# Two-layer hybrid encoder on one core: TensorE in emission order inside both attention stages

## The chip, the cores and the metric

The kernel runs on 1 core of one Trainium2 chip. The metric is the device time of one execution in microseconds (us); a kernel's time is the median over its runs.

## The reference

The program computes two transformer-like layers on a sequence of 1024 frames and 1024 channels. Each layer normalizes, mixes along the sequence, projects out with a gated residual, and runs a SwiGLU network. Only the mixers differ (cut):

```python
# layer 0
q, k, v, u = split(h @ w_in)
a_out = chunked_relpos_attention(q, k, v)   # 8 heads of 64, own + 8 earlier 64-frame chunks, softmax
b_out = s5_mixer(u)                         # complex diagonal scan, gelu, gate y * sigmoid(y @ w_glu)
x = x + g1 * (concat([a_out, b_out]) @ w_out)
x = x + g2 * swiglu(h2)
# layer 1
c_out = retention_mixer(cq, ck, cv, cg)     # 4 heads of 128, chunk recurrence, group norm, swish gate
d_out = stick_breaking_mixer(dq, dk, dv)    # 8 heads, 128-query blocks:
    # z = q @ k.T * scale; w = exp(log_sigmoid(z) + reverse cumsum of -softplus(z)); out = w @ v
x = x + g1 * (concat([c_out, d_out]) @ w_out)
x = x + g2 * swiglu(h2)
```

## The kernel before

All weights are multiplied at full precision by three passes: a weight tile is loaded as `raw` by SP, ACT casts it to its high part (line 141) and POOL or DVE subtracts to get the low part (line 142), into tiles named `whl` or `wo`; `mm3` then issues three matmuls per product (lines 248 to 250). PSUM has three tags: `mm` with 3 banks, `at` with 4, `av` with 1.

The program is written as generators on a clock of ticks (class Pipe, line 51). A generator yields a number n and is resumed n ticks later; a tick first resumes those that are due, in the order in which they were queued, then starts new ones. That sets the **emission order**: the order in which the program's text calls the instructions of each engine. Line 1541 opens the program with `schedule_with_timeline_sim=True`: a scheduler with its own simulated timeline then picks the order in which each engine gets its instructions. In the kernel before it does so for all engines, everywhere.

The first attention stage (`ab_phase`, layer 0) runs one a_unit a tick, for 64 pairs of head and 128-query block; the first three ticks lie in the stage before it. An a_unit is:

```python
sc, n = self.scores(self.mm_bank, ...)      # L498 on PE; L597, L600 on DVE: bias, row minimum
yield 1
nc.scalar.activation(pw, pw, AF.Exp, ...)   # L605 on ACT
yield 2
pts = self.flip(pool, pw, W // P)           # L510 transposes on PE, L512 copies on ACT
...                                         # even head: done
yield 1
self.weigh(av, ...)                         # L521 on PE, both heads of a pair
```

`weigh` is issued with the odd head alone, for both heads, and every fourth block ends with four transposes (L626) of a factor that POOL spreads (L619). Beside it an s5_block is started every fifth tick, 8 in all (L955 transposes of `u`, which a DMA brings, L964, L985, L987, L1002 on PE, most of the rest on DVE), and from step 46 on the gate's projection `glu`.

The second (`cd_phase`, layer 1) runs 32 periods of four ticks. Each period starts one d_unit (stick-breaking attention: query loads L483; four ticks later scores L498 into three `at` banks, mask add L1185 on DVE, two sigmoids L1188 and L1189 on ACT; one tick later two scans L1197 and a product L1199 on DVE; three ticks later nine transposes of `flip`; one tick later, odd heads, 18 matmuls of `weigh`) and one c_tile (retention: four ticks after its start a projection of 24 matmuls in four parts of one tick each; `ra`, `rb` on DVE, L1078 and L1079; `cr` on POOL, L1084; transposes L1089; `qkt`, `ckd` L1091 to L1094; L1097, L1099 on PE; `cat`, `cst`, L1101 and L1108, on DVE; L1112, L1114 on PE; statistics L1117, L1118 on DVE and L1119, L1120 on POOL; L1122 on DVE, which frees the `at` bank). Before it, `d_dense` (L1151) makes queries and keys, written to memory and loaded again from there.

Of the kernel before, what the change touches and what calls it, by code (L numbers as in the profile page):

```python
# [1368 lines left out]
def build(ctx, tc, I, out):  # L1369
    k = Trunk(ctx, tc, I, out)  # L1370
    nc, pipe = tc.nc, k.pipe
    k.cond()


    with tc.tile_pool(name="pp", bufs=1, reuse_waits="tile") as pp:
        with tc.tile_pool(name="first", bufs=1, reuse_waits="tile") as xp:
            k.first(pp, xp)
        with tc.tile_pool(name="heads", bufs=1, reuse_waits="tile") as hp:
            with tc.tile_pool(name="qk", bufs=1, reuse_waits="tile") as qp:
                right = ExitStack()  # L1380
                sp = right.enter_context(tc.tile_pool(name="set0", bufs=1, side="right", reuse_waits="tile"))
                k.stream.low = nc.vector
                for n, _ in enumerate(k.a_dense(qp)):
                    if n == 2:
                        setup = k.s5_setup(sp)
                        pipe.start(setup)
                    if n in (19, 32):
                        pipe.start(k.ada(qp, 0, 2 if n == 19 else 4))
                    if n == 38:
                        k.a_open(hp)  # L1390
                    if n == 46:
                        assert setup.gi_frame is None
                        right.close()
                        ap = right.enter_context(tc.tile_pool(name="mixa", bufs=1, side="right", reuse_waits="tile"))
                        k.pp = pp
                    pipe.tick(*([k.a_step(hp, ap, n - 46)] if n >= 46 else []))
                k.stream.low = nc.gpsimd
                pipe.tick(k.a_step(hp, ap, 2))
            k.ab_phase(hp, ap, 3)
            right.close()  # L1400
            k.pp = None
    with tc.tile_pool(name="xp0", bufs=1, reuse_waits="tile") as xp:
        x = [xp.tile([P, T], F32, name=f"x{n}") for n in range(NK)]
        for n in range(NK):
            nc.sync.dma_start(out=x[n], in_=I["x"][n])
        pipe.start(k.ada(xp, 0, 3))
        k.out_proj(xp, 0, x, [0, 1, 2, 4, 5, 6, 7, 3], 5, [(0, 4), (0, 3)], [k.ada(xp, 0, 5)])

        def done(n, h):
            if h:  # L1410
                nc.sync.dma_start(out=k.xd[n], in_=x[n])
            k.stat(xp, x[n], n, h)
            if n == NK - 1:
                pipe.start(k.norm(xp, x, h, [(1, 1), (1, 0)]))

        k.ffn(xp, 0, x, done, [lambda l=l, p=p: k.ada(xp, l, p) for l, p in ((1, 1), (1, 0), (1, 2), (1, 4), (1, 3))])
        for t in range(4):
            pipe.tick(k.v_tile(xp, "hf", k.wdv, t))
            pipe.tick()
        pipe.drain()  # L1420


    with tc.tile_pool(name="dense1", bufs=1, reuse_waits="tile") as dp:
        for n, _ in enumerate(k.d_dense(dp)):
            pipe.tick()
            if n == 1:
                for t in range(4, NT):
                    pipe.tick(k.v_tile(dp, "ve", k.wdv, t))
                    pipe.tick()
                k.wdv.free()  # L1430
    right = ExitStack()
    cp = right.enter_context(tc.tile_pool(name="mixc", bufs=1, side="right", reuse_waits="tile"))
    with tc.tile_pool(name="mixd", bufs=1, reuse_waits="tile") as dp:
        k.c_setup(cp)
        k.cd_phase(dp, cp)
    with tc.tile_pool(name="xp1", bufs=1, reuse_waits="tile") as xp:
        x = [xp.tile([P, T], F32, name=f"x{n}") for n in range(NK)]
        for kk in (0, 1, 2, 4, 5, 6):
            pipe.tick(k.mix_split(kk))
        pipe.tick(k.mix_split(3, 512))  # L1440
        for n in range(NK):
            nc.sync.dma_start(out=x[n], in_=k.xd[n])
        pipe.tick()
        while k.tail.gi_frame is not None:
            pipe.tick()
        right.close()
        k.out_proj(xp, 1, x, [0, 1, 2, 4, 5, 6, 7, 3], 1, [(1, 4), (1, 3)], [k.ada(xp, 1, 5)])

        def done(n, h):
            nc.sync.dma_start(out=out[n, :, h * 512:h * 512 + 512], in_=x[n][:, h * 512:h * 512 + 512])  # L1450

        k.ffn(xp, 1, x, done)
# [93 lines left out]
```

## Time and profile before

| | us |
|---|---|
| median of 3 runs | 2639.24 (2636.28 to 2641.58) |
| the profiled execution | 2628.13 |
| its span | 2626.3 |
| PE busy in the span | 2535.4 (97%) |
| PE weight loads busy | 2104.9 (80%) |
| DVE, ACT, POOL busy | 1134.9 (43%), 708.9 (27%), 809.5 (31%) |

The span is the time between the first and last instruction of the one profiled execution; 1.8 us of that execution lie around it. In the rows below, PE is TensorE's matmuls, PEld its weight loads (beside the matmuls), DVE VectorE, ACT ScalarE, POOL GpSimd, SP SyncE, which issues DMAs. A matmul with float32 operands has more records than instructions: each matmul of `weigh` shows as two.

### The profile page before, as it was taken

How to read it: one execution, taken by the hardware profiler on the slowest of the kernel's cores; microseconds unless marked ns; L12 is line 12 of the kernel's file. 1: busy time of each engine (PE TensorE's matmuls, PEld its weight loads, DVE VectorE, ACT ScalarE, POOL GpSimd, SP SyncE). 2: the span in 40 equal slices, each digit the busy share in tenths (PEclk: the TensorE clock that was granted, in tenths of full speed). 3: DMA queues.
4: the chain of work that ended last, by engine and by line, in shares of the span. 5: the costliest groups of instructions: out<-in, count | busy, mean ns of one | idle time of the engine just before them, and what ended most of it. 6: DMA issues, size and time to landing. Idle time of an engine off the chain costs nothing. (4 is left out here: it accounts for less than half of the span.)

```text
span 2626.3 us, 32531 instructions
## 1 busy us (share of the span) xinstructions
PE 2535.4 (97%) x12912; PEld 2104.9 (80%) x12912; DVE 1134.9 (43%) x2058; ACT 708.9 (27%) x1293; POOL 809.5 (31%) x538
## 2 busy tenths in 40 slices
PE   6999898999999999999999999999999999999999
PEld 4898776777888888888788778887788888888887
DVE  6576563474333322222531566765632222222223
ACT  4332568322111111111232444544231111111100
POOL 3465003423222222232212143423243333333311
PEclk9999999999999999999999999999999999999999
DMA  7287764543233311111234333224311111111101
GB/s 282 92 248 211 211 179 154 184 145 108 93 113 112 113 49 48 48 49 49 87 109 145 87 104 102 68 76 156 112 65 49 49 50 49 50 50 49 49 9 64
DMA packets 145479, 267.12 MB, mean 102 GB/s; under 512 B 34416, under 2 KB 82224, under 8 KB 144560
## 3 DMA queue, kind: packets, MB, share of 16 engines
q1 hardware_dynamic: 145328, 265.05, 31.7%
q8 instruction: 102, 1.67, 0.3%
q14 instruction: 49, 0.40, 0.1%
HBM read 221.22 MB, written 45.88 MB: 102 GB/s over the span
## 5 line engine op out<-in xcount | busy, mean ns | idle before, releaser
L249 PE MATMUL mm<-HT,whl 128*128 128x512 f32 x1744 | 680.3, 390 | 4.5 <-DVE HT L351 4.4
L248 PE MATMUL mm<-HT,whl 128*128 128x512 f32 x1744 | 680.7, 391 | 1.8 <-ACT HT L350 1.5
L250 PE MATMUL mm<-HT,whl 128*128 128x512 f32 x1744 | 679.8, 390 | 0.0
L142 POOL TENSOR_TENSOR whl<-raw,whl 128x1024 fp32r<-128x1024 f32 x136 | 332.5, 2453 | 494.5 <-ACT whl L141 487.8
L249 PEld LDWEIGHTS mm<-HT,whl 128*128 128x128 f32 x1744 | 327.7, 188 | 76.4 <-DVE HT L351 6.7
L248 PEld LDWEIGHTS mm<-HT,whl 128*128 128x128 f32 x1744 | 327.7, 188 | 72.8 <-ACT HT L350 2.8
L250 PEld LDWEIGHTS mm<-HT,whl 128*128 128x128 f32 x1744 | 327.9, 188 | 68.5
L1342 DVE SCALAR_TENSOR_TENSOR x<-at,col,x 128x512 f32<-128x512 f32 x352 | 262.4, 750 | 268.6 <-PE at L250 268.4
L1327 DVE TENSOR_TENSOR sg<-sg,mm 128x512 f32<-128x512 f32 x88 | 60.4, 687 | 642.3 <-PE mm L250 642.3
L249 PE MATMUL at<-aT,wo 128*128 128x512 f32 x704 | 274.9, 390 | 1.9 <-POOL aT L1329 1.9
L250 PE MATMUL at<-aT,wo 128*128 128x512 f32 x704 | 274.8, 390 | 0.0
L248 PE MATMUL at<-aT,wo 128*128 128x512 f32 x704 | 273.1, 391 | 0.0
L248 PE MATMUL mm<-whl,HT 128*128 128x512 f32 (+1 forms) x688 | 249.5, 363 | 8.6 <-ACT HT L402 8.1
L249 PE MATMUL mm<-whl,HT 128*128 128x512 f32 (+1 forms) x688 | 244.8, 356 | 0.0
L142 POOL TENSOR_TENSOR wo<-raw,wo 128x1024 fp32r<-128x1024 f32 x44 | 107.4, 2464 | 442.4 <-ACT wo L141 442.4
L250 PE MATMUL mm<-whl,HT 128*128 128x512 f32 (+1 forms) x688 | 242.1, 357 | 0.0
L141 ACT CAST whl<-raw 128x1024 fp32r<-128x1024 f32 x154 | 161.3, 1054 | 172.3 <-PE mm L250 164.7
L1329 POOL TENSOR_TENSOR aT<-sg,aT 128x512 fp32r<-128x512 f32 x88 | 115.2, 1309 | 289.6 <-DVE aT L1328 281.9
L1326 ACT ACTIVATE sg<-mm 128x512 f32<-128x512 f32 x88 | 52.6, 598 | 518.7 <-PE mm L250 518.7
L141 ACT CAST wo<-raw 128x1024 fp32r<-128x1024 f32 x44 | 44.0, 1046 | 494.2 <-PE at L250 488.0
L248 PEld LDWEIGHTS mm<-whl,HT 128*128 128x128 f32 x688 | 138.0, 201 | 25.7 <-ACT HT L402 10.7
L249 PEld LDWEIGHTS at<-aT,wo 128*128 128x128 f32 x704 | 132.2, 188 | 30.8 <-POOL aT L1329 2.4
(295 smaller groups left out, 3193.0 us busy)
## 6 DMA issues: line engine op xcount, KB each, us to landing
raw<-in_ffn_w_in SPq DMA_DIRECT2D x88, 512.0 KB, 3.5
raw<-in_ada_w SPq DMA_DIRECT2D x80, 512.0 KB, 4.0
raw<-in_ffn_w_out SPq DMA_DIRECT2D x44, 512.0 KB, 3.4
ada<-in_ada SPq DMA_DIRECT2D x16, 512.0 KB, 10.2
qkd<-stk SPq DMA_DIRECT2D x32, 256.0 KB, 4.8
q<-qkd SPq DMA_DIRECT2D x64, 128.0 KB, 3.9
ks<-qkd SPq DMA_DIRECT2D x32, 256.0 KB, 4.3
qkd<-stk SPq DMA_DIRECT2D x16, 512.0 KB, 3.2
```

The source lines that it names most:

```text
L141: nc.scalar.copy(hi, u.raw[:, :u.n])
L142: self.low.tensor_sub(lo, u.raw[:, :u.n], hi.bitcast(F32))
L248: mm(out, lhs.hi, rhs.hi, start=start, stop=False)
L249: mm(out, lhs.hi, rhs.lo, start=False, stop=False)
L250: mm(out, lhs.lo, rhs.hi, start=False, stop=stop)
L1326: nc.scalar.activation(sg, gu[0], AF.Silu)
L1327: nc.vector.tensor_mul(sg, sg, gu[1])
L1329: nc.gpsimd.tensor_sub(a[m].lo[:, sl], sg, a[m].hi[:, sl].bitcast(F32))
L1342: nc.vector.scalar_tensor_tensor(xh, ps, self.col[layer, 5][:, n:n + 1], xh, M, A)
```

## The change

Two calls are put into a context in which the order of one engine, PE, is not picked by the scheduler: it gets its instructions in emission order. All other engines are ordered by the scheduler as before, and so is PE outside of the two calls.

```diff
-            k.ab_phase(hp, ap, 3)
+            with tc.manual_schedule(engines={nc.tensor.engine}):
+                k.ab_phase(hp, ap, 3)
...
-        k.cd_phase(dp, cp)
+        with tc.manual_schedule(engines={nc.tensor.engine}):
+            k.cd_phase(dp, cp)
```

PE has the same matmuls in both kernels, and their order differs only in the two stages and in the first matmuls of the output projection behind each. Names with a number at the end are buffers; a row is an instruction, or several alike.

**Head of layer 1, PE.** `mm_10971` in the change is the last projection of d_dense; `mm_11216` before is the third of three projections of c_tiles (`mm_11064`, `mm_11127`, `mm_11216`, 72 matmuls in all, from which the last three stand here) that follow d_dense directly. Before:

```order
L248 MATMUL mm_11216<-whl_10904,HT_540 128x512
L249 MATMUL mm_11216<-whl_10904,HT_540 128x512
L250 MATMUL mm_11216<-whl_10904,HT_540 128x512
L498 MATMUL at_11047<-ks_11016,q_11038 128x128 x2
L498 MATMUL at_11053<-ks_11016,q_11038 128x512 x2
```

With the change:

```order
L248 MATMUL mm_10971<-HT_540,whl_10716 128x512
L249 MATMUL mm_10971<-HT_540,whl_10716 128x512
L250 MATMUL mm_10971<-HT_540,whl_10716 128x512
L498 MATMUL at_11052<-ks_11021,q_11043 128x128 x2
L498 MATMUL at_11058<-ks_11021,q_11043 128x512 x2
L498 MATMUL at_11061<-ks_11021,q_11043 128x512 x2
L248 MATMUL mm_11069<-whl_10780,HT_246 128x512
```

The first unit's scores moved from behind the 72 projection matmuls to ahead of them. SP's order up to the loads of that unit's queries is the same in both.

**Middle of layer 0, PE.** Before:

```order
L498 MATMUL mm<-ks,q 128x320 x2
L955 MATMUL at<-ident,u 128x128 x4
L521 MATMUL av<-pts,v 64x128
L498 MATMUL mm<-ks,q 128x320 x2
L521 MATMUL av<-pts,v 64x128 x5
L498 MATMUL mm<-ks,q 128x320 x2
L521 MATMUL av<-pts,v 64x128
L498 MATMUL mm<-ks,q 128x320 x6
```

With the change:

```order
L498 MATMUL mm<-ks,q 128x320 x4
L510 MATMUL at<-ident,pw 128x128 x5
L1002 MATMUL at<-ident,yg 128x128 x4
L498 MATMUL mm<-ks,q 128x320 x4
L510 MATMUL at<-ident,pw 128x128 x5
L521 MATMUL av<-pts,v 64x128 x10
```

Each weigh now stands in one piece; between the transposes of its own odd head and it stand one unit's scores and one unit's transposes. Over the whole program the matmuls of weigh stand in 101 separate runs before and in 49 with the change.

**A period of layer 1, PE.** `at_12306` is the third bank of scores of a d_unit, `mm_12419` a c_tile's projection. Before, the first two banks of these scores (`at_12297`, `at_12303`) stand ahead of that projection, and the third near its end:

```order
L249 MATMUL mm_12419<-whl_11907,HT_509 128x512
L498 MATMUL at_12306<-ks_11815,q_12211 128x448 x2
L250 MATMUL mm_12419<-whl_11907,HT_509 128x512
L510 MATMUL at_12327<-ident_69,b_12161 128x128 x4
L510 MATMUL at_12334<-ident_69,b_12161 128x128 x4
```

With the change, the same unit's three banks in a row:

```order
L498 MATMUL at_12302<-ks_11820,q_12216 128x256 x2
L498 MATMUL at_12308<-ks_11820,q_12216 128x448 x2
L498 MATMUL at_12311<-ks_11820,q_12216 128x448 x2
L248 MATMUL mm_12319<-whl_11033,HT_246 128x512
L249 MATMUL mm_12319<-whl_11033,HT_246 128x512
```

All three banks of scores are now issued together, ahead of the projection. Table loads on ACT, which its order shows too, are 16 before and 14 with the change.

**Head of layer 0, PE**, in words: before, 12 matmuls of scores, the transposes of `u` (L955), L964 and ten transposes of flips come before the first weigh. With the change the first weigh stands right behind L955, two matmuls of scores and three transposes; L964 and the rest follow it.

## Rows read from the trace of the kernel before

**Rows 1.** Windows by stretch: us, busy us of each engine, PEclk, DMA share, GB/s.

```profile
300.00:407.00 107.00, 97.72 (x815) 79.68 (x814) 73.07 (x266) 65.65 (x161) 5.01 (x5) 0.98 0.68 181
407.00:465.00 58.00, 50.76 (x334) 38.84 (x333) 17.63 (x59) 54.15 (x94) 23.94 (x17) 1.00 0.47 152
...
600.00:1000.00 400.00, 396.89 (x1778) 326.99 (x1778) 151.15 (x199) 57.08 (x68) 119.15 (x61) 1.00 0.29 92
1442.00:1458.00 16.00, 16.00 (x73) 13.24 (x72) 2.77 (x7) 3.68 (x7) 5.23 (x4) 1.00 0.83 222
1458.00:1482.00 24.00, 18.97 (x113) 15.27 (x112) 16.14 (x27) 12.14 (x31) 2.35 (x3) 0.86 0.19 54
1482.00:1792.00 310.00, 299.95 (x1891) 250.71 (x1890) 214.27 (x395) 150.05 (x372) 117.29 (x106) 0.98 0.28 83
```

**Rows 2.** Timeline of PE, head of layer 1: start us, us, instruction, idle before.

```profile
1442.30 0.39 PE L248 MATMUL mm<-whl,HT 128*128 128x512 f32 x1
...
1458.62 1.48 PE L498 MATMUL at<-ks,q 128*128 128x128 f32 x8
```

**Rows 3.** Line 483 on SP, 1450.5 to 1454.3: four query loads.

```profile
L483 SPq DMA_DIRECT2D q<-qkd x4: 574/586/614, 1450.8 to 1453.6; - x4
...
DMA to landing us min/median/max: 4.9/6.1/7.0
```

**Rows 4.** Timeline of PE at the head of layer 0.

```profile
279.43 1.11 PE L955 MATMUL at<-ident,u 128*128 128x128 f32 x4 [1.89 <-DMA u<-ud]
...
285.56 0.94 PE L521 MATMUL av<-pts,v 128*64 128x128 f32 x12
```

**Rows 5.** Line 487 on SP, 270 to 290: three value loads.

```profile
L487 SPq DMA_DIRECT2D v<-vd x3: 430/602/602, 279.0 to 284.2; - x3
...
DMA to landing us min/median/max: 4.8/4.8/5.4
```

**Rows 6.** Timeline of PE in layer 1: two runs of weigh.

```profile
1577.67 0.43 PE L521 MATMUL av<-pts,v 128*64 128x128 f32 x2
...
1578.25 0.98 PE L498 MATMUL at<-ks,q 128*128 128x384 f32 x4
...
1587.23 0.54 PE L521 MATMUL av<-pts,v 128*64 128x128 f32 x5
...
1589.34 0.97 PE L498 MATMUL at<-ks,q 128*128 128x384 f32 x4
```

**Rows 7.** Lines by shape, 300 to 407: busy us, mean ns.

```profile
L597 DVE CUSTOM_DVE_ANT_0 pw<-mm,abias 128x320 f32<-128x320 f32 x38 | 17.9, 483 | 4.0 <-PE mm L498 1.9 <-PE at L510 1.9
...
L605 ACT ACTIVATE pw<-pw,ast 128x640 f32<-128x640 f32 x18 | 14.9, 831 | 8.3 <-DVE ast L600 8.1
L512 ACT COPY pts<-at 128x512 f32<-128x512 f32 x24 | 13.9, 580 | 8.4 <-PE at L510 7.1 <-PE av L521 1.2
...
L512 ACT COPY pts<-at 128x128 f32<-128x128 f32 x24 | 6.3, 272 | 0.5 <-PE at L510 0.5
```

**Rows 8.** Lines of ACT, 407 to 465.

```profile
L605 ACT ACT_TABLE_LOAD x4 | 5.1, 1283 | 0.1
```

**Rows 9.** Lines of DVE and POOL, 1482 to 1792.

```profile
L1197 DVE TENSOR_TENSOR_SCAN w<-one,w 128x384 f32<-128x384 f32 (+7 forms) x56 | 82.6, 1475 | 19.7 <-ACT w L1188 19.6
...
L1084 POOL TENSOR_TENSOR cr<-ra,rb 128x256 f32<-128x256 f32 x28 | 43.1, 1540 | 180.7 <-DVE rb L1079 134.6 <-PE at L498 43.9 <-PE mm L521 2.1
...
L142 POOL TENSOR_TENSOR whl<-raw,whl 128x1024 fp32r<-128x1024 f32 x16 | 39.7, 2499 | 4.4 <-ACT whl L141 4.4
L1199 DVE TENSOR_TENSOR b<-b,w 128x1151 f32<-128x1151 f32 x28 | 37.7, 1348 | 0.5
...
L1094 DVE TENSOR_SCALAR ckd<-cr,c_kd 128x128 f32<-128x128 f32 x28 | 16.1, 574 | 0.8 <-POOL cr L1084 0.7
...
L1079 DVE TENSOR_TENSOR rb<-mm,ccs 128x256 f32<-128x256 f32 x28 | 11.5, 412 | 0.0
...
L1122 DVE TENSOR_SCALAR co<-at,cmv 128x128 f32<-128x128 f32 x28 | 11.3, 405 | 14.2 <-POOL cmv L1120 13.8
```

## Prediction, made before the change was run

> **What bounds the kernel now.** I read the windows of the two stages first, for what PE does there, then PE's timeline at the two heads of the stages and at two runs of `weigh`, then the rows of DVE, ACT and POOL from which a PE in a fixed order would have to wait.
>
> The windows show PE at work nearly all the time: 97.72 of 107 us in the middle of layer 0's attention, 50.76 of 58 in its second part, 299.95 of 310 in layer 1's [rows 1]. No other engine is full, except ACT in the second part of layer 0's (54.15 of 58) [rows 1]. So time is gained where PE's own time shrinks or its few idle microseconds go, and lost where PE stands before an instruction whose inputs are late while others behind it could run. The second is what a scheduler avoids and what a fixed order allows. Idle time of PE in these windows: 9.3 + 7.2 us in layer 0 and 10.0 in layer 1, 26.5 in all. A busy PE isn't a PE at its peak, so gains beyond the idle time are possible too.
>
> **The sum, part by part.** It stands against the profiled execution's 2628.13 us; the median of the runs shown is 2639.24, 11.1 us above it, and I add that at the end.
>
> 1. *Head of layer 1.* Before, d_dense is followed at 1442.30 by 72 projection matmuls of three c_tiles, and the first scores start at 1458.62 [rows 2]. Those scores read queries whose four loads SP issues from 1450.8 to 1453.6 and which land 4.9 to 7.0 us later, so about 1457 to 1458.5 [rows 3]. The projections thus fill just the time in which the queries are on their way: PE is busy for all of the 16 us [rows 1]. In the change the scores come directly behind d_dense. SP's order up to these loads is unchanged, and what SP waits for there (d_dense's results and free `raw` buffers) doesn't come sooner. PE then idles from 1442.5 to 1458.5: +16.0. The 72 matmuls come later and can cover what was open then: in 1458 to 1482 PE was busy for 18.97 of 24 us [rows 1], so 5.0 come back. **+11**. Bounds: +19, if nothing comes back and the loads land 3 later for DMAs that collide; +6, if the loads land 5 sooner, since the 72 matmuls no longer run beside d_dense's last evacuations and the weight casts.
>
> 2. *Head of layer 0.* Before, the transposes of `u` start when it lands, at 279.43, and the first weigh at 285.56 [rows 4]; its values are loaded from 279.0 on and land 4.8 us later, at 283.8 to 284.4 [rows 5]. Between the two PE issued scores, L964 and flips. In the change the first weigh stands right behind L955, so that some 30 matmuls which ran before the values landed come after: 12 of 320 to 512 columns, 8 of L964, 6 transposes, about 4 us. The loads of `u` and the values are issued one DMA (0.6 us) earlier. **+3**, bounds 0 to +6.
>
> 3. *Fewer runs of weigh.* Two weigh matmuls alone (two records each) take from 1577.67 to 1578.25, 0.58 us; sixteen in a run take 2.11 us, from 1587.23 to 1589.34 [rows 6]. The difference, 1.53, over the 14 more is 0.11 each, so that a run costs 0.36 us beyond its matmuls. The profile shows weigh on 128*64 tiles and its neighbours on 128*128. The change has 49 runs for 101, so 52 fewer. At 0.30 each, since some runs stand beside L964, which has 128*64 as well: **-16**; at 0.25 to 0.36, -13 to -19.
> The Trainium skill, TensorEngine Tiling (Array Packing), Key Properties, says that a change of the tiling mode drains TensorE. By it every run saved would be worth something, which speaks for this term; it gives no figure, and the term goes by the rows.
>
> 4. *Table loads.* Two of ACT's are gone, 1.28 us each [rows 8], in a stretch where ACT is at 93%: **-2.6**, 0 if ACT isn't waited for.
>
> 5. *Waits that the new order leaves.* The 26.5 us of idle PE in the windows [rows 1] are waits of the old order, and the old order is gone: **-26.5**; bound 0, if what is late (exp, reduction, sigmoids) is late in any order. I take them as gone because the new waits are counted from zero in the next part.
>
> 6. *Waits that the new order brings*, each behind one instruction on PE, with all of PE behind it:
>  - Weigh of layer 0. Between an odd head's transposes and its weigh stand one unit's four score matmuls (0.6 us) and five transposes (0.55). In that 1.15 us ACT must copy the transposes out, 0.58 + 0.27 = 0.85; if an exp of 0.83 is ahead, 1.68 [rows 7]. So 0 to 0.55 and latencies: 0.35 on each of 30, 10.5. Bounds 0 and 30 x 0.6 = 18.
>  - Scores of layer 0. They need a free `mm` bank; a reduction of 0.48 [rows 7] empties one and a unit takes two. DVE was busy 73 of 107 us [rows 1], with the s5 work ahead of the reduction at times. 0.13 on each of 57, 7.5; bounds 0 and 57 x 0.25 (half a reduction) = 14.
>  - Third bank of scores in layer 1. It is the bank that L1122 frees. From the end of a projection to there stand: `ra`, `rb` 0.82, `cr` 1.54, `ckd` 0.57, two scans 2.95, the product 1.35, L1122 0.41 [rows 9], and seven small instructions of DVE and POOL, at most 0.41 each, for which I take 0.34: 10.0 us. PE comes to it, after an even period, when it has issued the rest of that period: 24 projection matmuls at 0.225 (72 in 1442.30 to 1458.62 [rows 2]), 5.4; nine transposes, 1.0; three banks of scores, 1.0; six small ones, 1.2; and two banks of the next, 0.7: 9.3. So 0.7 on each of 16: 11. After an odd period PE has 18 weigh matmuls, 2 us, more to do, and doesn't wait. Bounds 0 and 16 x 1.1 (one more small DVE instruction ahead), 18. The scheduler has just this bank's matmuls half a period later.
>  - POOL's `cr` in layer 1. The subtraction of a weight tile, 2.50 us, stands 16 times among the 28 `cr` [rows 9]. Where it is ahead of one, `cr` and PE's L1089 are late by up to 2.5 less the slack of two ticks; 0.5 on each of 16, 8. Bounds 0 and 16.
>  Together **+37**, bounds 0 and +66.
>
> Sum: 11 + 3 - 16 - 2.6 - 26.5 + 37 = +5.9. On the median: 2639.2 + 5.9 = **2645 us**. All ends low: 6 + 0 - 19 - 2.6 - 26.5 + 0 = -42; all high: 19 + 6 - 13 + 0 + 0 + 66 = +78. Neither is likely, as the terms are independent.
>
> **The rivals.**
> - *The waits of part 6 stay small* (faster). Ticks give each dependence a fixed distance, and for all but the third bank the distance is about what the rows ask for. If half an exp or a subtraction is seldom in the way, 37 becomes 15: 5.9 - 22 = -16, **2623**. It decides from new waits of 31 us in all, 0.35 for each of 61 steps and 28 periods; below that the change gains. For it: ACT has 61% load in 300 to 407 and 48% in layer 1, DVE 68% and 69% [rows 1]. Against: their chains are long, and the idle rows show PE waiting already.
> - *PE's weight loads are the room* (faster). The windows show PEld at 118.5 of 165 us in layer 0, 72%, at 250.7 of 310, 81%, in layer 1, and at 327.0 of 400, 82%, in the dense work [rows 1]. If an order in large pieces lets both stages run as the dense work does, they take 118.5/0.82 = 144.5 and 250.7/0.82 = 305.7 us: -20 and -4; with both heads' +14, **2629**. The Trainium skill, Perfetto Trace Analysis, Identifying the Most-Contended Engine, says that weight-load busy time and not matmul busy time tells how much room TensorE has; by that rule layer 0 has more room than its 16.5 us of idle PE.
> - *Waits at their upper ends* (slower). The gate's stretch, where ACT has 93%, starves every weigh and the chain of the third bank meets POOL's subtractions: 66 for 37, +35, **2674**. It decides from 0.6 us per step.
> - *Even.* The heads cost 14 and the runs give 16; new waits equal the old ones, within 5 us: **2639**. 0.2%, 5.3 us, is about what a measurement of this kernel can tell from no change.
> - *The order isn't what bounds it*, so that all is hidden. PE's order is shown to change and PE is full, so 2 in 100.
>
> **How the numbers follow.** Forecast (+6 to +25) 0.30, waits small 0.25, room in the weight loads 0.11, even 0.21, upper ends 0.11, no effect 0.02. Faster: 0.25 + 0.11 = 0.36. Same: 0.21 + 0.02 = 0.23. Slower: 0.30 + 0.11 = 0.41. The signs are near even, so the range takes in both: down to **2617**, a little under the waits-small case, and up to **2669**, a little under the upper ends. The forecast alone would reach from 2643 to 2664.
>
> **What would show it.** Right, step by step: PE idle about 16 us before the first L498 of layer 1, released by a query DMA; a wait of the first L521 of layer 0 on a value DMA; PE waits at L521 on ACT L512, at L498 on DVE L597, at L498 of layer 1 on DVE L1122, some 16 of them of 0.7; runs of L521 in one piece that cost 0.3 beyond their matmuls; windows of the two stages in which PE's time is less by some 8 us each and its idle time about 10 us more. Wrong: the windows of both stages shorter with idle time below 26 us (then the first rival), or PEld over 80% in layer 0 (then the second), or a head without the 16 us.

## The result, and the profile after

| | before | with the change |
|---|---|---|
| median, us (runs) | 2640.41 (4) | 2658.38 (4) |
| lowest to highest, us | 2636.28 to 2643.53 | 2656.98 to 2661.75 |
| ratio | | 1.0071, 95% interval 1.0053 to 1.0088 |
| span of the profiled execution, us | 2626.3 | 2656.9 |
| mean granted clock of it | 0.992 | 0.981 |

The change makes the kernel slower by 18 us, 0.7%, and the whole interval (0.5 to 0.9%) lies above no change. The time is within the forecast's range, at three times the loss that was forecast (18 us for 5.9).

PE in the whole span, from the page (busy us, share, instructions). Before it was 2535.4 us:

```profile
PE 2527.8 (95%) x12912; PEld 2111.2 (79%) x12912; DVE 1142.6 (43%) x2058; ACT 702.8 (26%) x1291; POOL 788.4 (30%) x538
```

So PE was busy for 7.6 us less, in a span that is 30.6 us longer. Three of the windows of [rows 1] after the change, and 1442 to 1482 in one piece (us, busy time of PE, weight loads, DVE, ACT, POOL, then the granted clock, DMA share, GB/s):

```profile
300.00:407.00 107.00, 89.76 (x779) 75.03 (x777) 66.82 (x249) 63.06 (x153) 4.82 (x5) 0.97 0.69 178
407.00:465.00 58.00, 43.14 (x300) 35.29 (x301) 19.78 (x73) 43.41 (x81) 18.25 (x12) 0.88 0.52 159
1442.00:1482.00 40.00, 24.13 (x107) 19.65 (x105) 3.46 (x5) 7.98 (x10) 9.50 (x4) 0.86 0.60 172
1482.00:1792.00 310.00, 295.85 (x1903) 252.06 (x1904) 219.41 (x395) 143.73 (x373) 91.64 (x101) 0.97 0.28 81
```

In 300 to 407 PE has 17.2 us without work, where [rows 1] had 9.3; in 407 to 465 14.9 for 7.2, with the clock at 0.88; at the head of layer 1 15.9 of 40. Layer 1's body is near the old one, 14.2 for 10.0. (The windows are the same times, not quite the same work: layer 1 starts some 24 us later in the change.)

The two heads. Before, PE's order had other work there [rows 2, 4]; now its timeline (start, duration, instruction, idle time before it and what ended it) shows the stalls. Layer 0, then layer 1:

```profile
278.82 1.12 PE L955 MATMUL at<-ident,u 128*128 128x128 f32 x4 [5.79 <-DMA u<-ud]
...
284.81 0.69 PE L521 MATMUL av<-pts,v 128*64 128x128 f32 x2 [3.80 <-DMA v<-vd]
```

```profile
1482.54 2.56 PE L498 MATMUL at<-ks,q 128*128 128x128 f32 x6 [16.41 <-DMA q<-qkd]
```

What PE waited for (total us, times, longest), in layer 0's attention, 268 to 480:

```profile
PE mm L248 <- ACT whl L141: 7.2, 1, 7.2
PE at L985 <- DVE x L703: 6.2, 6, 1.5
PE at L955 <- DMA u<-ud: 5.8, 1, 5.8
PE at L985 <- DVE x L700: 5.3, 2, 3.3
PE av L521 <- ACT pts L512: 4.5, 4, 1.9
PE av L521 <- DMA v<-vd: 4.0, 2, 3.8
...
PE mm L249 <- POOL whl L142: 1.6, 1, 1.6
...
PE mm L498 <- DVE ast L597: 0.2, 1, 0.2
```

and in layer 1's, 1436 to 1840:

```profile
PE at L498 <- DMA q<-qkd: 16.4, 1, 16.4
PE at L498 <- DVE co L1122: 9.7, 3, 3.2
PE at L1089 <- POOL cr L1084: 4.7, 1, 4.7
PE at L1089 <- DVE cst L1108: 2.0, 8, 0.3
```

Look at which instructions lead. The scores of layer 0 (last row of the first list) and the wait of layer 1's scores for queries were priced, and so were L521's waits for ACT and L1122 and `cr` in layer 1; the scan block's L985 (11.5 us in eight waits) and the gate's first projection (7.2 + 1.6 us) were not.

**Where the time went**, split by the profile alone. PE's span is idle time, plus work at full clock, plus what working at 1.2 GHz costs. Idle is the span less PE's busy time; the windows of the stretches at 1.2 GHz give PE's busy time in them, and half of that is the cost of the lower clock: a 128x512 matmul of L248 takes 0.39 us at full clock [rows 2] and 0.80 at 433.28 in the change, in a stretch at 1.2 GHz. In the change those stretches add up to 102.4 us with PE busy for 75.2, so 37.6 us.

| profiled execution of | span | idle | cost of 1.2 GHz | the rest: work at full clock |
|---|---|---|---|---|
| before | 2626.3 | 90.9 | 18.3 | 2517.1 |
| before, a second one | 2635.8 | 92.4 | 27.7 | 2515.7 |
| the change | 2656.9 | 129.1 | 37.6 | 2490.2 |
| layer 0 alone (a_only) | 2651.0 | 111.8 | 34.6 | 2504.6 |
| layer 1 alone (d_only) | 2639.1 | 108.4 | 31.0 | 2499.7 |

Emission order does shorten PE's work, by 26 us. It pays 37 us in idle time (some 20 more in layer 0's attention and 18 in layer 1's, a little less elsewhere) and 10 (against the second execution of before) to 19 us in time at the lower clock.

### The profile page after: what moved, and what is told of

Read it like the earlier page. It is cut to its first block, busy times and chain, and to the rows that moved or that the text cites. A ratio compares the mean times of both kernels' runs of the same rounds, so it can differ in the third digit from the quotient of the medians.

```text
span 2656.9 us, 32549 instructions
## 1 busy us (share of the span) xinstructions
PE 2527.8 (95%) x12912; PEld 2111.2 (79%) x12912; DVE 1142.6 (43%) x2058; ACT 702.8 (26%) x1291; POOL 788.4 (30%) x538
## 4 chain that ended last, share of the span: by engine, by line
PE 78%; DVE 9%; DMA 5%; issue 3%; ACT 2%; POOL 2%; SPq 1%; DVEq 0%; ACTq 0%; POOLq 0%
PE mm L248 17%; PE mm L249 17%; PE mm L250 17%; PE at L249 6%; PE at L248 6%; PE at L250 6%; DMA raw<-in_ada_w 2%; PE av L521 1%; PE at L510 1%; DVE ada L288 1%; DVE w L1197 1%; POOL whl L142 1%; PE at L498 1%; PE mm L521 1%; DVE HT L351 1%
## 5 line engine op out<-in xcount | busy, mean ns | idle before, releaser
L248 PE MATMUL mm<-HT,whl 128*128 128x512 f32 x1744 | 681.8, 392 | 0.9 <-ACT HT L350 0.9
L248 PEld LDWEIGHTS mm<-HT,whl 128*128 128x128 f32 x1744 | 328.3, 188 | 71.5 <-ACT HT L350 2.0
L248 PE MATMUL at<-aT,wo 128*128 128x512 f32 x704 | 273.1, 391 | 0.0
L248 PE MATMUL mm<-whl,HT 128*128 128x512 f32 (+1 forms) x688 | 256.0, 372 | 9.3 <-ACT HT L402 8.1
L249 PE MATMUL mm<-whl,HT 128*128 128x512 f32 (+1 forms) x688 | 246.4, 358 | 0.0
L250 PE MATMUL mm<-whl,HT 128*128 128x512 f32 (+1 forms) x688 | 243.3, 359 | 0.0
L248 PEld LDWEIGHTS mm<-whl,HT 128*128 128x128 f32 x688 | 139.1, 202 | 28.0 <-ACT HT L402 10.7
```

Source lines behind the costliest of these rows:

```text
L248: mm(out, lhs.hi, rhs.hi, start=start, stop=False)
L249: mm(out, lhs.hi, rhs.lo, start=False, stop=False)
L250: mm(out, lhs.lo, rhs.hi, start=False, stop=stop)
```

## The experiments

All timed comparisons are against the kernel before on the same chip.

**The kernel before, again (before_again).** No edit.

> The kernel before without an edit, for a second profiled execution: the first one was 11 us under the median of the timed runs. Theory 1: the same as before, ratio within 0.9985 to 1.0015, and where its profile differs from the first by about 11 us shows in which stretch the executions of this kernel vary. Theory 2: the profile is again near 2628 us and the timed runs are longer than profiled ones throughout.

Measured: 2635.79 us for 2636.25, ratio 0.9989 (0.9975 to 1.0003). Its profiled span is 2635.8, 9.5 us longer than the first. Idle time and work agree within 1.5 us (table above); the time at 1.2 GHz is 64.9 us for 41.0, and 9.4 us of the 9.5 is that cost. Theory 1: the two executions differ by the clock, not by a stretch of work.

**One stage alone (a_only, d_only).**

```diff
-            k.ab_phase(hp, ap, 3)
+            with tc.manual_schedule(engines={nc.tensor.engine}):
+                k.ab_phase(hp, ap, 3)
```

> Emission order in layer 0's attention alone; layer 1 is left to the scheduler. In the trace of the change the first SwiGLU activation of layer 0 starts 23.6 us later than in the trace of the kernel before, and the stretch from there to the same point of layer 1 is 7.1 us longer. Theory 1 (the stages add up, and layer 0 carries most of the loss): 11 to 24 us slower than the kernel before, ratio 1.004 to 1.009. Theory 2 (layer 0's 23.6 us is in part chance of one profiled execution, and layer 1's wait for queries is the main loss): under 6 us, ratio below 1.0025.

```diff
-        k.cd_phase(dp, cp)
+        with tc.manual_schedule(engines={nc.tensor.engine}):
+            k.cd_phase(dp, cp)
```

> Emission order in layer 1's attention alone; layer 0 is left to the scheduler. Theory 1: the 16.4 us wait of PE for the first queries stands again, the periods behind it are 0.6 us shorter each, and the sum is +7 us, ratio 1.001 to 1.005. Theory 2: +12 us or more, ratio 1.0045 or above, since the periods gain nothing of their own.

Measured: layer 0 alone 2654.10 us, ratio 1.0061 (1.0039 to 1.0084), 16 us; layer 1 alone 2641.42 us, ratio 1.0018 (1.0003 to 1.0032), 5 us. They add up to 21 for the 18 of both. Theory 1 in both: layer 0 carries three quarters of the loss, as far as intervals of 0.15 to 0.23% to either side tell.

**Layer 1 with its head left to the scheduler (d_from4).** The context is entered before period 4, so the first four periods are free and the 72 projections stand ahead of the first scores again.

```diff
         for n in range(32):
+            if n == 4:
+                man.enter_context(self.tc.manual_schedule(engines={self.nc.tensor.engine}))
```

> As emission order in layer 1's attention alone, but only from its fifth period on; the first four are left to the scheduler, so that 72 projection matmuls stand again ahead of the first scores. Theory 1 (the wait for queries is all that layer 1 loses, and it is not given back later): no wait above 2 us for the first queries, and 16 us less than emission order in all of layer 1, so 6 to 12 us faster than the kernel before, ratio 0.9955 to 0.998. Theory 2 (the 72 matmuls only change places, and what is saved at the head is lost behind it): within 3 us of emission order in all of layer 1.

Measured: 2641.05 us, ratio 1.0014 (0.9997 to 1.0031): not 16 us less than layer 1 in full, but the same. The wait for queries is gone (17.0 us in d_only). The last weigh matmul starts 360.8 us after d_dense's last activation, for 369.0 in d_only: 8 us were gained up to there, half of the wait; the 72 projections that stood behind it no longer fill the gaps that follow, and L510 waits for L1199, as in the kernel before and not in the change. The wait for L1122 stays (PE, 1436 to 1840):

```profile
PE at L498 <- DVE co L1122: 10.8, 4, 3.2
...
PE at L510 <- DVE b L1199: 3.9, 1, 3.9
```

Behind the stage the profiled execution loses the 8 us again, with 10.2 us at 1.2 GHz from 1893.8 on, behind the output projection, that d_only's hasn't; among the kernels here some profiles have it (before_low) and some not (both of before). The time is Theory 2's, and its account holds for half of the wait by the last weigh; where the other half goes is seen in one profile only. In the timed runs the head is worth nothing that can be told.

**Layer 1 with head and tail left to the scheduler (d_4_28).** The same, and `if n == 28: man.close()`.

> Layer 1's attention in emission order from its fifth to its 28th period alone, with head and tail left to the scheduler. With emission order from the fifth period to the end PE waits 10.8 us at the third bank of scores for L1122, 4.7 us for cr in the last period and 1.8 us behind the stage. Theory 1: the last two go, 5 us less than with emission order to the end, so the same as the kernel before or up to 3 us faster, ratio 0.9985 to 1.001. Theory 2 (time at 1.2 GHz takes it back): as emission order from the fifth period to the end, ratio 1.001 to 1.003.

Measured: 2637.30 us for 2635.73, ratio 1.0001 (0.9988 to 1.0013). Theory 1: emission order in the middle of layer 1 is even with the scheduler's.

**Layer 0, three of its waits, one at a time.** (Lines behind the edit are 4 to 6 higher in some of these kernels.) The interval of layer 0 alone reaches from 1.0039 to 1.0084, and those of the next four kernels all overlap it, so no single time here is clear of it; what each edit does is read from the traces. First the head left to the scheduler (a_from6: the context entered at `n == 6`).

> Emission order in layer 0's attention alone, from the seventh tick of the phase on; the first six are left to the scheduler. With emission order in all of layer 0's attention PE waits 5.8 us for u and 4.9 us for the values at the head; the kernel before waits 5 us there in all. Theory 1 (the loss of layer 0 is a sum of separate waits): the head's waits fall to 5 us and the kernel is about 5 us faster than with emission order in all of layer 0 (2654 us), ratio to the kernel before 1.003 to 1.005. Theory 2 (the head is made up for later, and the loss is at the gate): 2654 us within 3, ratio 1.005 to 1.007.

Measured: 2651.63 us, ratio 1.0042 (1.0029 to 1.0055). In 268 to 607 PE's waits for `u` and for the values fall to 2.7 us, from 10.7 in a_only, and one for queries, 2.5, comes in, so that 5.2 are left, near the 4.6 of the kernel before; the gate's is as in a_only:

```profile
PE mm L248 <- ACT whl L141: 7.2, 1, 7.2
...
PE mm L498 <- DMA q<-qkd: 2.5, 1, 2.5
...
PE av L521 <- DMA v<-vd: 1.5, 1, 1.5
...
PE at L959 <- DMA u<-ud: 1.2, 1, 1.2
```

By the two ratios 5 us less than layer 0 in full, by the medians 2.5: Theory 1 in the trace, and in the time as far as the noise lets it be seen.

Then the gate's stretch left to the scheduler (a_0_44: the context closed at `n == 44`).

> Emission order in layer 0's attention up to the 44th tick of the phase; the gate's stretch behind it is left to the scheduler. With emission order in all of it PE waits 8.5 us for the first gate weight (6.9 on ACT's cast, 1.6 on POOL's subtraction) and 4.1 us for copied transposes there. Theory 1 (separate waits): these go, and the kernel is 8 to 13 us faster than with emission order in all of layer 0, ratio to the kernel before 1.001 to 1.003. Theory 2 (the scan block's waits on DVE are the main loss): under 5 us faster, ratio 1.004 or above.

Measured: 2650.88 us, ratio 1.0045 (1.0031 to 1.0058); 3 to 4 us less, for the 8 to 13 of Theory 1. The wait for the gate's weight fell from 6.9 us to 1.3:

```profile
PE mm L248 <- ACT whl L141: 1.3, 1, 1.3
```

Idle time fell by 8.9 us against a_only, but PE's work at full clock grew by 6.5 (2511.1 for 2504.6). The scheduler fills the waits by cutting the work into smaller pieces: layer 0's weigh stands in 43 runs for 35. That this is what the work grew by wasn't tried. It is Theory 2's time by another way.

Then the scan block's output one tick later (a_s5).

```diff
-        yield 4
+        yield 5
         yb = self.at_bank()
...
-            if n == 46:
+            if n == 47:
```

> Emission order in layer 0's attention alone, and the scan block's output matmuls (L985, L987) stand one tick later than before (five ticks behind the products that they read, for four); the gate starts one tick later for it. With emission order in all of it PE waits 12.2 us at L985 for DVE's last product, eight times. Theory 1 (DVE is late by up to 2.7 us, about a tick): this wait falls below 3 us, and the kernel is 6 to 10 us faster than with emission order alone, ratio to the kernel before 1.002 to 1.004. Theory 2 (DVE is the bound of these ticks, whatever stands where): PE waits as long at another instruction for DVE, and the time stays within 3 us of 2654, ratio 1.005 to 1.007.

Measured: 2649.62 us, ratio 1.0040 (1.0026 to 1.0053), 5.5 us less by the ratios. The 12.2 us at L985 are gone, and PE waits longer at other places:

```profile
PE mm L248 <- ACT whl L141: 6.2, 1, 6.2
PE av L521 <- ACT pts L512: 6.0, 4, 3.2
...
PE at L510 <- DVE t L971: 3.1, 2, 1.7
```

L510 for DVE's scan products is new there (3.1 us), L521 went from 4.1 to 6.0, and the gate's weight is late as before. So a part of both: 12.2 us of waits are removed, and idle time falls by 5.9 (105.9 for 111.8).

Last, the gate four ticks later (a_glu50).

```diff
-            if n == 46:
+            if n == 50:
```

> Emission order in layer 0's attention alone, and the gate starts four ticks later (at tick 50 of the phase for 46). Theory 1 (the 8.5 us wait for the gate's first weight is a matter of distance, the weight comes through memory from the scan's result): the wait is gone; the gate's projections reach four ticks further behind the last attention step, where they stand in one piece; 5 to 9 us faster than emission order alone, ratio to the kernel before 1.002 to 1.0045. Theory 2 (what is saved at its start is lost at its end, as nothing of attention is left beside its ACT and POOL work): within 3 us of 2654, ratio 1.005 to 1.007.

Measured: 2661.20 us, ratio 1.0085 (1.0071 to 1.0099): 6 to 7 us slower than without the edit, by the middle values, which neither theory had. The wait for the gate's weight is gone from the list, but the stage from the first scores to the first SwiGLU activation takes 350.6 us for 334.4. The last steps' weigh and transposes now wait for an ACT that has the gate's work beside theirs, with 3.7 us at L510 and at L521

```profile
PE av L521 <- ACT pts L512: 9.1, 6, 4.1
```

**All three together (mid_s5).** Head and gate's stretch left to the scheduler (context from `n == 6` to `n == 44`), and the later scan output.

> Layer 0's attention in emission order from tick 6 to tick 44 alone, with its head and its gate stretch left to the scheduler, and the scan block's output matmuls one tick later; layer 1 is left to the scheduler. Theory 1 (the loss of layer 0 is the sum of the waits at the head, at L985 and at the gate, each with the time at 1.2 GHz that follows it): all three are gone, and the shorter runs of weigh and fewer idle gaps show: 0 to 8 us faster than the kernel before, ratio 0.997 to 1.000. Theory 2 (emission order itself, in the middle of the stage, leaves waits that move from one instruction to the next): still 5 us or more slower, ratio above 1.002.

Measured: 2636.41 us for 2635.73, ratio 1.0002 (0.9988 to 1.0016). The 16 us of layer 0 are gone with the three waits, but no gain is left: PE's idle time is 98.7 us, its work 2507.1, the cost of the clock 34.0, for 92.4, 2515.7 and 27.7 of before. What the order saves in work, 9 us, its last waits and the clock take. This ratio is clear of that of layer 0 alone, so the loss lies in these three places together; two of them were given back to the scheduler, so the run doesn't show that emission order can do without the waits there.

**POOL's subtraction out of layer 1 (d_low).** In the change's trace the third bank of scores waits 3.2 us for L1122. PE, then POOL and DVE (start, duration, instruction) at one of the three:

```profile
1652.16 1.22 PE L498 MATMUL at<-ks,q 128*128 128x512 f32 x2 [3.23 <-DVE co L1122]
```

```profile
1643.61 3.08 POOL L142 TENSOR_TENSOR whl<-raw,whl 128x1024 fp32r<-128x1024 f32 x1 [2.92 <-ACT whl L141]
1648.48 0.22 POOL L1119 TENSOR_SCALAR cmv<-cmv 128x1 f32<-128x1 f32 x1 [1.79 <-DVE cmv L1118]
1648.78 2.35 POOL L142 TENSOR_TENSOR whl<-raw,whl 128x1024 fp32r<-128x1024 f32 x1
1651.09 0.57 POOL L1120 TENSOR_TENSOR cmv<-cmv,mhalf 128x1 f32<-128x1 f32 x1
...
1654.75 2.36 POOL L142 TENSOR_TENSOR whl<-raw,whl 128x1024 fp32r<-128x1024 f32 x1
1657.07 3.27 POOL L1133 TENSOR_TENSOR ce<-ce,cg 128x512 f32<-128x512 f32 x1
```

```profile
1643.01 1.49 DVE L1197 TENSOR_TENSOR_SCAN w<-one,w 128x640 f32<-128x640 f32 x1
1644.60 3.31 DVE L1199 TENSOR_TENSOR b<-b,w 128x1151 f32<-128x1151 f32 x1
...
1651.70 0.41 DVE L1122 TENSOR_SCALAR co<-at,cmv 128x128 f32<-128x128 f32 x1 [2.45 <-POOL cmv L1120]
...
1655.12 4.14 DVE L1197 TENSOR_TENSOR_SCAN w<-one,w 128x1024 f32<-128x1024 f32 x1 [0.66 <-ACT w L1188]
...
1668.77 2.29 DVE L1197 TENSOR_TENSOR_SCAN w<-one,w 128x1024 f32<-128x1024 f32 x1
1671.17 1.36 DVE L1199 TENSOR_TENSOR b<-b,w 128x1151 f32<-128x1151 f32 x1
```

L1122 needs POOL's L1119 and L1120, and between these two stands a subtraction of a weight tile, 2.35 us; it's the same at the two other waits. There is more in these rows. While POOL subtracts at 1643.61, DVE's product L1199 takes 3.31 us (1.36 at 1671.17); the statistics that L1119 reads stand behind it on DVE, so that this subtraction delays L1122 as well, by 2 us. And beside the subtraction of 1654.75 and POOL's product L1133 a scan of 1024 columns takes 4.14 us (2.29 at 1668.77). The Trainium skill, SBUF — State Buffer, Who interferes with whom, says that a DVE instruction with two inputs in SBUF contends with a GpSimd instruction that reads SBUF; L1199 reads two such inputs, and the rows agree. So the subtraction was moved, on top of d_4_28:

```diff
         k.c_setup(cp)
+        k.stream.low = nc.vector
...
         pipe.tick()
+        k.stream.low = nc.gpsimd
         while k.tail.gi_frame is not None:
```

> As emission order from the fifth to the 28th period of layer 1, and in that stage the low part of a weight tile (L142) is subtracted on DVE and not on POOL. In the trace of the change each wait of PE for L1122 (3.2 us, three times) has a subtraction of 2.4 us on POOL between the two POOL instructions that L1122 needs. Theory 1 (POOL's subtraction is what makes the third bank late): these waits fall from some 10 us to under 2, DVE's 16 subtractions of 1.4 us move other DVE work by less than PE notices, and the time is 4 to 8 us less than without this edit. Theory 2 (DVE's chain is what makes it late, as the prediction had it): the waits stay or grow, as DVE has 23 us more to do, and the time is the same or longer.

Measured: 2622.75 us for 2635.73, ratio 0.9946 (0.9932 to 0.9961): 13 us faster than before, and 14.5 than d_4_28. The waits for L1122 were 10.8 us and are

```profile
PE at L498 <- DVE co L1122: 1.1, 1, 1.1
```

and 0.7 us at L510. Theory 1, at twice its price. The stage from d_dense's last activation to the first SwiGLU activation is 457.5 us for 474.4 in d_4_28; PE's idle time in it is 22.8 us for 28.6, and 10.2 us are at 1.2 GHz for 34.1. The edit removes both ways in which the subtraction delays L1122, and doesn't tell them apart.

**The same edit in the kernel before (before_low).** The two lines alone; the scheduler orders PE everywhere.

> The kernel before, ordered by the scheduler everywhere, with one edit: in layer 1's attention stage the low part of a weight tile is subtracted on DVE and not on POOL. Emission order with this edit is 13 us faster than the kernel before, and without it even. Theory 1 (the fixed order needs it, and the scheduler already puts other work into POOL's delay): 0 to 5 us faster than the kernel before, ratio 0.998 to 1.000; emission order in the middle of layer 1 is then worth 8 us or more. Theory 2 (the delay by POOL costs either order the same, with the time at 1.2 GHz behind it): 10 to 15 us faster, ratio 0.994 to 0.9965, and the emission order is worth nothing beyond it.

Measured: 2621.66 us for 2638.75, ratio 0.9935 (0.9914 to 0.9956): 17 us faster than the kernel before, and the fastest here. Theory 2, a little above its price: the gain belongs to the edit, and emission order adds nothing to it. The scheduler orders PE anew with the edit (its matmuls stand in another order in this stage), so its part is in the gain. Its old order had been paying as well, at another place. Before (second execution), then with the edit, PE's waits in 1436 to 1840:

```profile
PE at L1089 <- ACT b L1189: 9.8, 7, 2.3
```

```profile
PE at L1089 <- ACT b L1189: 0.5, 3, 0.2
```

Why L1189 is late in the old order and not in the new wasn't followed further.

The second stage takes 457.3 us there for 468.4, with 10.0 us idle for 20.3. That is 11 of the 16 us by which the two profiled spans differ; most of the rest lies in layer 0's attention (316.4 for 322.2, and 315.0 in the first execution of before), which the edit doesn't touch.

## Why the prediction was right in its sign, and where its sum was off

The range took in both signs, with 0.41 on slower, so that a time inside it proves little; the forecast's own span, 2643 to 2664, holds the time too. By its parts:

1. *Head of layer 1, +11.* The wait came as foreseen, 16.4 us on the queries of [rows 3]. 5 us were to come back, for a cost of 11; by the last weigh d_from4 shows a cost of 8. Right, and 3 us too dear.
2. *Head of layer 0, +3.* The waits are 5.8 us for `u` and 4.0 for the values, 9.8, where the kernel before waited 4.6 (2.7 for queries, 1.9 for `u`). That is 5.2 more, within the bounds, and 2.5 to 5 in time by a_from6. Right.
3. *Fewer runs of weigh, -16.* PE's work at full clock fell by 26 us, 11 in layer 0 and 16 in layer 1 (table). Not all of it is the runs. Windows of one line alone show which matmuls are shorter (us, busy time of PE and of its weight loads in that line). Weigh, L521, in the whole span, in the second execution of before and in the change, then the scores of layer 1, L498, in the same two:

```profile
0.00:2660.00 2660.00, 96.15 (x1056) 70.89 (x1056) 0.99 0.32 100
```

```profile
0.00:2660.00 2660.00, 76.10 (x1056) 62.29 (x1056) 0.98 0.32 100
```

```profile
1000.00:2660.00 1660.00, 51.30 (x192) 30.70 (x192) 0.99 0.22 70
```

```profile
1000.00:2660.00 1660.00, 42.48 (x192) 33.38 (x192) 0.99 0.22 71
```

 Weigh is 20 us shorter, 0.39 for each of the 52 runs, an estimate since records of neighbours overlap: near the 0.36 read and the 0.30 taken, so the term was right, if a little small. The scores of layer 1, whose three banks stand in a row now, are 8.8 us shorter, for which the prediction had no term. That the pieces are the cause is argued and wasn't tried.
4. *Table loads, -2.6.* Nothing shows it; ACT is the late engine at the gate for another reason, below. Not tried alone.
5. *Old waits gone, -26.5, and* 6. *new waits, +37.* Here the sum was off in size. PE's idle time rose by 37 us in all (129.1 for 92.4), for the 24.5 of the two heads and these two terms. The waits of weigh and scores in layer 0, priced at 18, are 4.5 and 0.2. The two that were not priced are 11.5 and 8.8. Layer 0's new waits thus come to 25 for 18, at other instructions than those priced; that they are no further off is luck:
 - L985 waits for DVE's products of the scan block, whose chain has four ticks; the longest wait is 3.3 us. The prediction listed the block and never laid its chain against its ticks, as it did for the third bank.
 - The gate's first projection waits for a weight that is a result of the scan, written to memory and read back. PE, then ACT, then SP at that place:

```profile
433.28 0.80 PE L248 MATMUL mm<-whl 128*128 128x512 f32 x1 [7.15 <-ACT whl L141]
```

```profile
431.10 1.06 ACT L140 ACTIVATE raw<-raw 128x1024 f32<-128x1024 f32 x1 [3.44 <-DMA raw<-ytd]
432.19 1.04 ACT L141 CAST whl<-raw 128x1024 fp32r<-128x1024 f32 x1
```

```profile
424.69 0.55 SPq L1005 DMA_DIRECT2D ytd<-yt  x1
...
427.16 0.38 SPq L130 DMA_DIRECT2D raw<-ytd  x1
```

 The result is stored at 424.69, the load issued at 427.16, ACT starts on it at 431.10 (after waiting 3.4 us for it), casts at 432.19, and PE starts at 433.28, its low part's matmul at 435.72. Before, PE had attention's and other matmuls to do meanwhile.
 - In layer 1 the third bank and POOL's `cr` were priced at 19 together; their waits are 9.7 and 4.7, with 2.0 at L1089 besides. The size was right and the cause half wrong: not 16 times 0.7 by DVE's chain, but three times 3.2, where POOL's subtraction stands between L1119 and L1120 and another delays L1199. d_low shows that it was POOL's subtraction.
7. *The clock.* No term had it. The time at 1.2 GHz rose from 41.0 and 64.9 to 102.4 us, and cost 10 to 19 us more. Idle time gained less work saved is 11 us against either execution of before, so that the clock is about half of the loss or more. In the timed runs the mean granted clock is 0.980, for 0.988 over the executions of before.

The rivals: *even* is out, as the interval begins at 14 us. The weight-load rival is refuted (PEld 75.0 of 107 in 300 to 407, less than the 79.7 of [rows 1], and neither stage ran shorter). The rival with small waits was right for attention's own chain in layer 0 alone. The slower rival lies 16 us above the result, the forecast 13 below; of its mechanism the starved weigh shows with 4.5 us only, but the chain of the third bank did meet POOL's subtractions, in the three waits of 3.2 us.

## What to carry to other kernels

Fixing one engine's order takes away the one freedom that hides late inputs: lay every chain that crosses engines against its distance in that order, above all those outside the main loop (a block that starts every few steps, a weight that comes back through memory, the first loads of a stage). Price a wait of TensorE above its length, since the work behind it may run at the lower clock. And ask which other engine makes both orders wait: the two lines that moved a subtraction from POOL to DVE were worth 17 us (12 to 23 by the interval), more than any order here.

## What the runs showed of the hardware

**The granted clock sets how two executions of one kernel differ.** Those of the kernel before differ by 9.5 us, and 9.4 of it is the cost of the time at 1.2 GHz. Most of those stretches begin after TensorE stood idle or had little to do (in the change one, at 221.1, begins after full work), as here, where the wait for the third bank ends at 1739.9 (us, busy time of the engines, the granted clock third from the end):

```profile
1736.10:1740.10 4.00, 0.76 (x4) 0.32 (x4) 1.54 (x6) 3.14 (x8) 3.78 (x4) 1.00 0.44 143
1740.10:1743.50 3.40, 3.40 (x9) 2.64 (x10) 2.74 (x3) 1.08 (x2) 3.40 (x3) 0.50 0.51 177
```

PE is busy for 0.8 of 4 us, and its work in the next row runs at the lower clock throughout. The Trainium skill, TensorE: Matmul & The Clock Gate, HAM oscillation — how this bites in real kernels, tells the same of waits for loads: the work that follows starts at half speed. A stretch can lie mostly in the wait itself and cost little: of the 17.1 us at 1.2 GHz at the head of layer 1 PE is busy for 4.9. And the time at 1.2 GHz changes from one execution to the next, so a term for it is an average.

**A product or scan on DVE waits for a subtraction on POOL that is already running.** The subtraction of 1643.61 ends at 1646.69; the product L1199, started beside it, ends 1.2 us later, near the 1.36 that it takes alone. So it looks like a wait until POOL has ended, and not like work at half speed. The two overlap four times in layer 1 of the change, and L1199 takes 3.3 us each time; 24 others, with nothing on POOL beside them, take 1.35 to 1.36. The scan of 1655.12 likewise ends 2.15 us after the subtraction of 1654.75, and takes 2.29 alone. It goes the other way too: the subtraction of 1643.61 itself started beside a scan (1643.01), which takes its usual 1.49, and took 3.08 for 2.35; POOL's L1133 beside the scan of 1655.12 takes 3.27, and 1.27 to 1.31 in the kernel before. In the kernel before, moving the subtraction shortens all 64 scans of the stage together from 94.0 to 89.1 us, and DVE is busy for 304.3 us in it (304.9 before), though it has 21.6 us of subtractions more.
